# A hybrid streaming layer: four steps moved from VectorE to ScalarE and TensorE, and one set of weight parts made once

## The chip, the cores and the metric

The kernel runs on one core of a Trainium2 chip. The metric is the device time of one execution in microseconds (us). TensorE (PE in the profile) does the matmuls, VectorE (DVE), ScalarE (ACT) and GpSimd (POOL) the elementwise work; SyncE (SP) issues most of the DMAs. Each engine takes its own instructions in the order in which they were planned.

## What is computed

One layer of a streaming encoder in fp32, for 1024 prompt tokens and 8 running streams of 16 tokens each (1152 tokens in all, width 1024): RMSNorm, one input projection to three mixers, an output projection with a residual, RMSNorm, SwiGLU, a residual and a last RMSNorm. The mixers and the two parts that the change touches, cut:

```python
def rglru(x, h0, ...):                       # mixer A
    log_a = -LRU_C * r * softplus(-lam)
    a = exp(log_a)
    u = sqrt(-expm1(2.0 * log_a)) * (i * x)
    # h[t] = a[t] * h[t-1] + u[t]; then y = h * gelu(gate)

def ssd_chunk(s, inp):                       # mixer B
    acs = cumsum(da, axis=1)
    diff = acs[:, :, None] - acs[:, None]
    decay = exp(where(causal_mask, diff, -inf))
    cb = einsum("btgn,bsgn->btsg", cm, bm)
    y = einsum("btsg,btsgh,bsghp->btghp", cb, decay, x) + ...
    s_new = exp(acs[:, -1]) * s + einsum("bsgn,bsghp->bghpn", bm, x * tail)

def trunk_layer(x, ...):
    x = x + einsum("bte,ed->btd", mix, w_out)
    h2 = rmsnorm(x, norm2_w)                 # y * rsqrt(mean(x*x) + eps)
    ff = silu(h2 @ w_ffn_gate) * (h2 @ w_ffn_up)
    x = x + ff @ w_ffn_down
```

## The kernel before

Tokens lie in nine tiles of 128; tile 0 (`samp`) holds the eight running streams, tiles 1 to 8 the prompt. Three tiles are a chunk of 384 columns. Every fp32 operand of a large matmul is split into a high part (fp32r, copied by ACT) and a low part (the rest, a subtraction on DVE or POOL), and a product is three matmuls (`mm3`, L144 to L146). Weights come by `load_w` (L159 loads, L160 high part, L164 low part), or, in the feed-forward, by `a_parts`, where `split` (L179, L180) makes the parts and L1008 to L1011 combine blocks of the weights before.

The stages, in program order: the first norm and the input projection for all tokens; `mix_c` for each tile (mixer C); `mix_a` twice (mixer A, halves of its width); `proj_xbc` and `proj_z` (inputs of mixer B); then per chunk three times `mix_b` and, between them, `w_out` for the chunk (output projection, residual, squares for the second norm); then the feed-forward.

`mix_a` works on tiles of 128x1152. After an exponential (L358) and a tanh (L359) on ACT, L361 makes `0.5 t + 0.5` of the first on DVE, L362 to L365 go on, L367 makes `-2 t - 1` on DVE ahead of the scan. The gelu of the gate has one such step too (L381, `0.044715 t + 1`).

`mix_b` has for each of the two groups of four heads a tile `L` of 128x512 that a DMA fills with the cumulated decays along the free side (`ad`, broadcast). Four DVE instructions (L721), one for a head, subtract the decay of the partition's own token and cut at 0; ACT takes the exponential of all four (L722), DVE multiplies by the masked C B (L723). In the sample tile a loop over eight sequences follows: DVE copies a strip (`zw`, L734), two matmuls read the old state (`pi`), DVE masks B to the sequence (`bm`, L739, one buffer), two matmuls give the new contribution (`pn`, tag c of PSUM, three banks, of which `pi` holds two), POOL scales the old state (L743) and DVE adds (L744).

`w_out(c)` has eight output tiles of 24 matmuls of 384 columns (`pw`, two banks of tag a). For each, DVE adds the residual (L819), a DMA stores it, and `add_sq` takes the square on ACT (L216, L219) and adds it on DVE to a running sum (L220). After the eighth, `row_scale` sums over partitions by three matmuls of one column (`pss`), DVE and POOL take the power -1/2, and a matmul with a diagonal spreads it (`rrow`).

The feed-forward takes tokens in two sets, s = 1 (640 tokens, matmuls of 320 columns) and s = 0 (512 tokens, 256 columns), and hidden features in 11 pairs of tiles. Each block product is done in seven products instead of eight (Strassen's way), in this order: A11, S2, S3, S4, A12, S1, A22. `build(s)` makes the seven combinations of the tokens, first the high and low parts of three, then of four (L979, L984, L180). `build(1)` needs the first two chunks alone, `build(0)` needs the last. So pair 0 is done apart: `gate_up(0, (1,), "0a")`, `build(0)`, `gate_up(0, (0,), "0b")`; each call makes the gate's weight parts (g0a, g0b) and then the up's (u0a, u0b). Three buffers each hold high and low parts, so a set of parts takes the place of the one before as the products let go of it. From pair 1 on one set of parts serves both s. The down projection is last.

The order of the instructions on each engine is planned by a list scheduler on a simulated timeline; code under `feed()` or `high_priority` is taken ahead.

Of the kernel before, what the change touches and what calls it, by code (L numbers as in the profile page):

```python
# [18 lines left out]
P = 128  # L19
# [34 lines left out]
AE = dict(g0a="101", u0a="010", g0b="101", u0b="010")  # L54
# [36 lines left out]
def hybrid_step(ctx, tc, xT, xTp, vec, rows, nrow, wch, wtk0, wtk1, wout, wgate, wup, wdown,  # L91
# [28 lines left out]
    V.memset(cst[:, 2:3], float(np.exp(1.0)))  # L120
    ident, ones = cio[:, 0:P], cio[:, P:2 * P]
# [77 lines left out]
    def row_scale(rs, sq, c, name):  # L199

        load_cm()
        pc = bank("d", f"pss{name}", [TPC])
        for i in range(TPC):
            for j, x in enumerate(sq):
                mm(pc[:, i:i + 1], x[:, i * P:(i + 1) * P], ones[:, 0:1], j == 0, j == len(sq) - 1)
        rstd_from(rs, pc, D)
# [138 lines left out]
    def mix_a(j):  # L345
# [15 lines left out]
        V.tensor_scalar(t4, t4, 0.5, 0.5, ALU.mult, ALU.add)  # L361
# [5 lines left out]
        V.tensor_scalar(t3, t3, -2.0, -1.0, ALU.mult, ALU.add)  # L367
# [13 lines left out]
        V.tensor_scalar(t4, t4, 0.044715, 1.0, ALU.mult, ALU.add)  # L381
# [299 lines left out]
    def mix_b(t, last):  # L681
# [122 lines left out]
    def w_out(c):  # L804
        mT = st["mT", c]
        cs = slice(c * CH, (c + 1) * CH)
        sq = io.tile([P, CH], F32, tag="sq", name=f"sq2{c}", bufs=SQ)
        for m in range(KD):
# [14 lines left out]
        row_scale(r, [sq], c, f"2{c}")  # L823
# [71 lines left out]
    etb = pr.tile([P, NB, 8], F32, name="etb")  # L895

# [90 lines left out]
    def a_parts(w, pair, name, single):  # L987
# [34 lines left out]
    def gate_up(pair, ss, tag):  # L1022
        gt = {s: pg.tile([P, 2, 2, BN[s]], F32, tag=f"g{s}", name=f"g{s}_{tag}") for s in ss}
        for w, up in ((wgate, False), (wup, True)):
            nm = f"{'gu'[up]}{tag}"
            tm = {}
            for s in ss:
# [62 lines left out]
    for pair in range(1, NF // 2):  # L1090
        gate_up(pair, (0, 1), str(pair))
# [345 lines left out]
```

## Time and profile before

| | us |
|---|---|
| median of 3 runs (lowest to highest) | 1451.86 (1448.03 to 1453.65) |
| the profiled execution's own time | 1447.59 |
| its span in the trace | 1445.8 |
| busy in the span: TensorE, VectorE, ScalarE, GpSimd | 1349.6, 1082.0, 523.2, 527.2 |
| mean granted TensorE clock | 0.976 of full |

The span is the time between the first and the last instruction of the program; the rest of the execution's time lies around it. Matmuls are pipelined, so two of them overlap in the trace, and the step from one start to the next is what one costs in a row. Idle time of an engine is told with what ended it. TensorE's clock is granted at one of two levels, 1.2 or 2.4 GHz, and a stretch shows the mean as a share of the higher.

### The profile page before, as it was taken

How to read it: one execution, taken by the hardware profiler on the slowest of the kernel's cores; microseconds unless marked ns; L12 is line 12 of the kernel's file. 1: busy time of each engine (PE TensorE's matmuls, PEld its weight loads, DVE VectorE, ACT ScalarE, POOL GpSimd, SP SyncE). 2: the span in 40 equal slices, each digit the busy share in tenths (PEclk: the TensorE clock that was granted, in tenths of full speed). 3: DMA queues.
4: the chain of work that ended last, by engine and by line, in shares of the span. 5: the costliest groups of instructions: out<-in, count | busy, mean ns of one | idle time of the engine just before them, and what ended most of it. 6: DMA issues, size and time to landing. Idle time of an engine off the chain costs nothing.

```text
span 1445.8 us, 24385 instructions
## 1 busy us (share of the span) xinstructions
PE 1349.6 (93%) x9341; PEld 1299.9 (90%) x9341; DVE 1082.0 (75%) x2016; ACT 523.2 (36%) x895; POOL 527.2 (36%) x419
## 2 busy tenths in 40 slices
PE   8998998999988899787899999999999999999986
PEld 7898887899987799787899999999999999998885
DVE  8475697988777697689556666565666688999896
ACT  7332255444533145464322231232222453333222
POOL 4160032211014332213543454544545433452453
PEclk9999999999999999988999999999999999999998
DMA  6263131433466887750412322223322363544523
GB/s 236 77 209 125 42 101 52 125 106 103 135 221 215 274 280 257 235 188 30 153 47 99 117 102 102 69 78 116 103 100 90 111 208 109 178 134 127 166 66 131
DMA packets 107289, 195.82 MB, mean 135 GB/s; under 512 B 10845, under 2 KB 66597, under 8 KB 107045
## 3 DMA queue, kind: packets, MB, share of 16 engines
q1 hardware_dynamic: 102276, 186.40, 39.0%
q0 software_dynamic: 4896, 7.87, 1.9%
q8 instruction: 73, 1.20, 0.3%
q14 instruction: 44, 0.35, 0.1%
HBM read 137.82 MB, written 56.41 MB: 134 GB/s over the span
## 4 chain that ended last, share of the span: by engine, by line
PE 53%; DVE 27%; DMA 9%; issue 5%; ACT 3%; POOL 3%; SPq 0%; DVEq 0%; POOLq 0%; ACTq 0%
PE pS_g L144 3%; PE pS_u L144 3%; PE pS_u L145 3%; PE pS_g L146 3%; PE pS_g L145 3%; PE pS_u L146 3%; PE pA_u L144 2%; PE pA_u L146 2%; PE pA_u L145 2%; PE pA_g L145 2%; PE pA_g L144 2%; PE pA_g L146 2%; DVE as L180 2%; PE pmb L145 2%; PE pmb L144 2%
## 5 line engine op out<-in xcount | busy, mean ns | idle before, releaser
L144 PE MATMUL pd<-e,as 128*128 128x256 f32 (+1 forms) x560 | 167.3, 301 | 9.8 <-ACT as L179 4.7
L146 PE MATMUL pd<-e,as 128*128 128x256 f32 (+1 forms) x560 | 162.6, 298 | 3.1 <-DVE as L180 3.1
L145 PE MATMUL pd<-e,as 128*128 128x256 f32 (+1 forms) x560 | 165.1, 296 | 0.0
L144 PEld LDWEIGHTS pd<-e,as 128*128 128x128 f32 x560 | 106.4, 190 | 14.2 <-ACT as L179 6.1
L180 POOL TENSOR_TENSOR al_u<-wr_u,ah_u 128x1024 fp32r<-128x1024 f32 x30 | 72.1, 2404 | 117.1 <-ACT ah_u L179 117.1
L146 PEld LDWEIGHTS pd<-e,as 128*128 128x128 f32 x560 | 105.3, 190 | 4.7 <-DVE as L180 4.6
L145 PEld LDWEIGHTS pd<-e,as 128*128 128x128 f32 x560 | 105.9, 189 | 0.1
L180 POOL TENSOR_TENSOR al_g<-wr_g,ah_g 128x1024 fp32r<-128x1024 f32 x30 | 71.9, 2396 | 90.5 <-ACT ah_g L179 89.8
L179 ACT ACTIVATE ah_g<-wr_g 128x1024 fp32r<-128x1024 f32 x30 | 31.8, 1062 | 150.8 <-PE pS_u L145 80.4
L1046 POOL TENSOR_TENSOR g<-g,pt_u 128x256 f32<-128x256 f32 (+1 forms) x80 | 76.9, 980 | 20.3 <-DVE pt_u L1045 15.4
L146 PE MATMUL pA_g<-b,al_g 128*128 128x256 f32 (+1 forms) x240 | 71.5, 299 | 1.6 <-POOL al_g L180 1.6
L144 PE MATMUL pw<-mT,wh_o 128*128 128x384 f32 x192 | 67.5, 354 | 4.9 <-DVE xr L819 4.2
L144 PE MATMUL pA_g<-b,ah_g 128*128 128x256 f32 (+1 forms) x240 | 71.6, 298 | 0.4 <-ACT ah_g L179 0.4
L145 PE MATMUL pA_g<-b,ah_g 128*128 128x256 f32 (+1 forms) x240 | 71.5, 298 | 0.0
L144 PE MATMUL pS_g<-b,ah_g 128*128 128x256 f32 (+1 forms) x240 | 70.9, 296 | 0.5 <-ACT ah_g L179 0.5
L144 PE MATMUL pA_u<-b,ah_u 128*128 128x256 f32 (+1 forms) x240 | 71.0, 296 | 0.0
L146 PE MATMUL pA_u<-b,al_u 128*128 128x256 f32 (+1 forms) x240 | 70.8, 295 | 0.0
L144 PE MATMUL pS_u<-b,ah_u 128*128 128x256 f32 (+1 forms) x240 | 70.6, 295 | 0.0
L145 PE MATMUL pA_u<-b,ah_u 128*128 128x256 f32 (+1 forms) x240 | 70.6, 294 | 0.0
L145 PE MATMUL pS_g<-b,ah_g 128*128 128x256 f32 (+1 forms) x240 | 70.6, 295 | 0.0
L146 PE MATMUL pS_u<-b,al_u 128*128 128x256 f32 (+1 forms) x240 | 70.5, 294 | 0.0
L145 PE MATMUL pS_u<-b,ah_u 128*128 128x256 f32 (+1 forms) x240 | 70.4, 294 | 0.0
(725 smaller groups left out, 4779.2 us busy)
## 6 DMA issues: line engine op xcount, KB each, us to landing
wr_o<-in_dram SPq DMA_DIRECT2D x24, 512.0 KB, 4.9
wr_g<-in_dram SPq DMA_DIRECT2D x20, 512.0 KB, 3.5
wr_u<-in_dram SPq DMA_DIRECT2D x20, 512.0 KB, 3.5
wd<-in_dram SPq DMA_DIRECT2D x15, 512.0 KB, 4.2
wr_t<-in_dram SPq DMA_DIRECT2D x14, 512.0 KB, 3.6
fr<-ffd SPq DMA_DIRECT2D x11, 640.0 KB, 4.0
ffd<-g SPq DMA_DIRECT2D x10, 640.0 KB, 2.9
ffd<-g SPq DMA_DIRECT2D x10, 512.0 KB, 3.0
```

The costliest lines, as they stand in the source:

```text
L144: T.matmul(out, ah, bh, start=start, stop=False)
L145: T.matmul(out, ah, bl, start=False, stop=False)
L146: T.matmul(out, al, bh, start=False, stop=stop)
L179: S.activation(dst_hi, src, AF.Copy)
L180: eng.tensor_tensor(dst_lo, src, dst_hi.bitcast(F32), ALU.subtract)
L1046: G.tensor_tensor(g, g, u, ALU.mult)
```

## The change

Five edits.

1. In `mix_b` the decay differences are made by ACT: `relu(acs - L)`, with the token's own decay as the bias per partition, and the exponential takes the scale -1.
2. In the sample tile's loop B is masked twice ahead of the loop, once for the even and once for the odd sequences (`par`), and the matmul for a sequence reads the 32 rows in which it and its neighbour lie.
3. In `mix_a` the three steps L361, L367 and L381 go to ACT as `Identity` with a bias.
4. In `w_out` of the last chunk each square goes into one of two buffers, and three matmuls of one column add it in PSUM, in a bank for each of the three token tiles (one of tag b, two of c); the running sum on DVE goes.
5. In pair 0 the order is now gate for s = 1, up for s = 1, `build(0)`, up for s = 0 with the same weight parts, gate for s = 0. So u0b, its loads and its parts go, and the gate's silu for s = 0 comes after the up.

```diff
-        V.tensor_scalar(t4, t4, 0.5, 0.5, ALU.mult, ALU.add)
+        S.activation(t4, t4, AF.Identity, bias=cst[:, 1:2], scale=0.5)
...
-        V.tensor_scalar(t3, t3, -2.0, -1.0, ALU.mult, ALU.add)
+        S.activation(t3, t3, AF.Identity, bias=cst[:, 3:4], scale=-2.0)
...
-        V.tensor_scalar(t4, t4, 0.044715, 1.0, ALU.mult, ALU.add)
+        S.activation(t4, t4, AF.Identity, bias=ones[:, 0:1], scale=0.044715)
...
-                V.tensor_scalar(L[:, h, :], L[:, h, :], acs[:, hh:hh + 1], 0.0, ALU.subtract, ALU.min)
-            S.activation(L, L, AF.Exp)
+                S.activation(L[:, h, :], L[:, h, :], AF.Relu, bias=acs[:, hh:hh + 1], scale=-1.0)
+            S.activation(L, L, AF.Exp, scale=-1.0)
...
         if samp:
+            bm = [pr.tile([P, 2, P], F32, tag=("ke", "oc")[e], name=f"bm{e}") for e in range(2)]
+            for e in range(2):
+                V.tensor_scalar(bm[e], Bt, par[:, e:e + 1], None, ALU.mult)
             for b in range(NB):
                 s0 = st["s0f"][:, b, :]
+                rs = slice(b // 2 * 32, b // 2 * 32 + 32)
...
-                bm = pr.tile([P, 2, P], F32, tag="ke", name=f"bm{b}")
-                V.tensor_scalar(bm, Bt, seqm[:, b:b + 1], None, ALU.mult)
                 pn = bank("c", f"pn{b}", [8, 64])
                 for g in range(2):
-                    mm(pn[:, g * 4:g * 4 + 4, :], bm[:, g, :], xq[:, g * 4:g * 4 + 4, :])
+                    mm(pn[:, g * 4:g * 4 + 4, :], bm[b % 2][rs, g, :], xq[rs, g * 4:g * 4 + 4, :])
...
+        if c == NCHUNK - 1:
+            pcs = [bank("bcc"[i], f"pss2{c}{i}", [1]) for i in range(TPC)]
...
                 V.tensor_tensor(xr, xr, pm, ALU.add)
                 dma(x1d[:, m, cs], xr)
-                add_sq(sq, xr, m, f"2{c}", V)
+                if c == NCHUNK - 1:
+                    tq = io.tile([P, CH], F32, tag=("tq", "sq")[m % 2], name=f"tq2{c}_{m}", bufs=1)
+                    S.activation(tq, xr, AF.Square)
+                    for i in range(TPC):
+                        mm(pcs[i], tq[:, i * P:(i + 1) * P], ones[:, 0:1], m == 0, m == KD - 1)
+                else:
+                    add_sq(sq, xr, m, f"2{c}", V)
...
             def out(s, i, h, x, pm):
                 g, u = gt[s][:, i, h, :], tm[s][0]
-                if up:
-                    V.tensor_tensor(u, x, pm, ALU.add)
+                o = u if second else g
+                V.tensor_tensor(o, x, pm, ALU.add)
+                if not up:
+                    S.activation(o, o, AF.Silu)
+                if second:
                     G.tensor_tensor(g, g, u, ALU.mult)
-                else:
-                    V.tensor_tensor(g, x, pm, ALU.add)
-                    S.activation(g, g, AF.Silu)
...
+            for sp in sps:
+                second = sp[0] in gt
+                if up and pair == 0 and sp == (0,):
+                    build(0)
...
-    gate_up(0, (1,), "0a")
-    build(0)
-    gate_up(0, (0,), "0b")
+    gate_up(0, ((0, "g0a", ((1,),)), (1, "u0a", ((1,), (0,))), (0, "g0b", ((0,),))))
     for pair in range(1, NF // 2):
-        gate_up(pair, (0, 1), str(pair))
+        last = pair == NF // 2 - 1
+        gate_up(pair, ((0, f"g{pair}", ((0, 1),)), (1, f"u{pair}", ((0,), (1,)) if last else ((0, 1),))))
```

## Rows read from the trace of the kernel before

**Rows 1.** The page's first part: busy time, share, instructions.
```profile
PE 1349.6 (93%) x9341; PEld 1299.9 (90%) x9341; DVE 1082.0 (75%) x2016; ACT 523.2 (36%) x895; POOL 527.2 (36%) x419
```
**Rows 2.** Busy us by stretch: length, PE PEld DVE ACT POOL, clock, DMA share, GB/s.
```profile
180.00:290.00 110.00, 99.90 (x572) 89.35 (x572) 99.14 (x184) 59.10 (x117) 29.66 (x32) 0.95 0.31 94
396.00:440.00 44.00, 39.85 (x327) 38.53 (x326) 32.93 (x81) 17.40 (x39) 6.36 (x7) 1.00 0.70 233
440.00:490.00 50.00, 38.18 (x229) 32.42 (x227) 39.49 (x75) 10.72 (x21) 22.09 (x21) 1.00 0.70 228
490.00:598.00 108.00, 101.41 (x596) 96.74 (x596) 77.89 (x158) 46.38 (x90) 33.18 (x35) 0.97 0.86 277
598.00:640.00 42.00, 32.63 (x175) 31.52 (x173) 41.16 (x53) 24.43 (x37) 5.04 (x2) 0.94 0.50 160
640.00:704.00 64.00, 51.72 (x332) 50.09 (x332) 52.94 (x78) 27.87 (x39) 28.42 (x14) 0.85 0.29 103
704.00:1250.00 546.00, 543.46 (x4070) 542.35 (x4071) 362.43 (x617) 163.25 (x268) 260.14 (x171) 1.00 0.32 107
```
**Rows 3.** Waits of PE, 598 to 724 us: us in total, times, longest.
```profile
PE pss L139 <- DVE sq L220: 6.5, 1, 6.5
PE pS_u0a L144 <- ACT ah_u0a L179: 5.3, 1, 5.3
...
PE pS_g0b L146 <- DVE s1p_g0b L180: 2.4, 1, 2.4
PE pS_g0b L144 <- ACT ah_g0b L179: 1.9, 1, 1.9
...
PE pS_u0b L144 <- ACT ah_u0b L179: 1.1, 1, 1.1
PE pS_u0b L146 <- DVE s1p_u0b L180: 0.9, 1, 0.9
```
**Rows 4.** Busy time by stretch: sum of six at the lower clock.
```profile
sum 34.13, PE 27.30 PEld 27.00 DVE 26.27 ACT 10.94 POOL 13.66; mean PE 4.55 PEld 4.50 DVE 4.38 ACT 1.82 POOL 2.28
```
**Rows 5.** Groups of instructions, DVE, 598 to 704 us: busy, mean ns, idle before.
```profile
L220 DVE TENSOR_TENSOR sq<-sq,tq 128x384 f32<-128x384 f32 x7 | 3.9, 552 | 0.0
```
**Rows 6.** Timeline, DVE, 665 to 685 us: start, us, instruction.
```profile
665.49 0.68 DVE L1008 TENSOR_TENSOR s_g0b<-wr_g0b 128x512 f32<-128x512 f32 x1
...
680.54 2.83 DVE L180 TENSOR_TENSOR s1p_g0b<-s_g0b,s1p_g0b 128x512 fp32r<-128x512 f32 x1
683.69 1.21 DVE L180 TENSOR_TENSOR b<-xb,b 128x1024 fp32r<-128x1024 f32 x1
```
**Rows 7.** Timeline, PE, 702 to 703 us: two matmuls in a row.
```profile
702.42 0.28 PE L144 MATMUL pA_u0b<-b,ah_u0b 128*128 128x256 f32 x1
702.54 0.28 PE L145 MATMUL pA_u0b<-b,ah_u0b 128*128 128x256 f32 x1
```
**Rows 8.** Timeline, PE, 57 to 60 us: the one-column matmuls of a chunk.
```profile
57.44 0.72 PE L139 MATMUL pss<-cio,xk 128*128 128x1 f32 x6
```
**Rows 9.** Waits of PE, 396 to 612 us.
```profile
PE pn L139 <- DVE bm L739: 5.0, 5, 1.7
...
PE ptz L145 <- DVE wl_t L164: 3.1, 1, 3.1
```
**Rows 10.** Line L739: count, duration in ns (min/median/max), first and last start.
```profile
L739 DVE TENSOR_SCALAR bm<-ws,cm x8: 341/348/1448, 447.0 to 486.5; 128x256 f32<-128x256 f32 x8
```
**Rows 11.** Timeline, DVE, 404 to 407 us: four heads, with the wait before.
```profile
404.75 0.87 DVE L721 TENSOR_SCALAR ws<-ws,sml 128x128 f32<-128x128 f32 x4 [3.62 <-DMA ws<-acd]
```
**Rows 12.** Timeline, ACT, 176 to 184 us: two in a row with bias.
```profile
182.50 0.69 ACT L561 ACTIVATE ke<-ldq 128x128 f32<-128x128 f32 x2
```
**Rows 13.** Line L361 on DVE: count, duration in ns, first and last start.
```profile
L361 DVE TENSOR_SCALAR a<-a x2: 751/754/756, 185.4 to 233.7; 128x1152 f32<-128x1152 f32 x2
```
**Rows 14.** Groups by form, ACT: an affine step with exponential.
```profile
L358 ACT ACTIVATE a<-a,sp 128x1152 f32<-128x1152 f32 x2 | 2.7, 1342 | 0.0
```
**Rows 15.** Groups by form, ACT: the table loads of L364.
```profile
L364 ACT ACT_TABLE_LOAD x2 | 2.6, 1283 | 0.0
```

More of the change, by code (lines that the diff above doesn't have):

```diff
@@ L53 @@
 SEQ = "4abcd7856"
-AE = dict(g0a="101", u0a="010", g0b="101", u0b="010")
+AE = dict(g0a="101", u0a="010", g0b="101")
 SEN = ((1, 0), (1, 0), (1, 0))
@@ L120, in hybrid_step @@
     V.memset(cst[:, 2:3], float(np.exp(1.0)))
+    V.memset(cst[:, 3:4], -1.0)
     ident, ones = cio[:, 0:P], cio[:, P:2 * P]
@@ L201, in row_scale @@
         load_cm()
[L202 to L206, printed above, removed]
+        if sq is None:
+            powc(rs, rs, 0)
+        else:
+            pc = bank("d", f"pss{name}", [TPC])
+            for i in range(TPC):
+                for j, x in enumerate(sq):
+                    mm(pc[:, i:i + 1], x[:, i * P:(i + 1) * P], ones[:, 0:1], j == 0, j == len(sq) - 1)
+            rstd_from(rs, pc, D)
         dg = io.tile([P, CH], F32, tag="tq", name=f"dg{name}", bufs=TQ)
@@ L806, in w_out @@
         cs = slice(c * CH, (c + 1) * CH)
-        sq = io.tile([P, CH], F32, tag="sq", name=f"sq2{c}", bufs=SQ)
+        if c == NCHUNK - 1:
+            pcs = [bank("bcc"[i], f"pss2{c}{i}", [1]) for i in range(TPC)]
+        else:
+            sq = io.tile([P, CH], F32, tag="sq", name=f"sq2{c}", bufs=SQ)
         for m in range(KD):
@@ L895, in hybrid_step @@
     etb = pr.tile([P, NB, 8], F32, name="etb")
+    par = pr.tile([P, 2], F32, name="par")
+    V.tensor_reduce(par, seqm.rearrange("p (i e) -> p e i", e=2), mybir.AxisListType.X, ALU.add)
     f0, f1, q0 = first_tiles(("f0", "f1", "q0"), ws)
@@ L985, in build, with a_parts @@
             split(b_part(s, k, 0, 3, 4), b_part(s, k, 1, 3, 4), t, V)
-    def a_parts(w, pair, name, single):
+    def a_parts(w, pair, name):
         def pairs(src, nm, eng=G):
@@ L1020, in a_parts, with gate_up @@
                     A22=half(g1, 1), S2=half(g2, 0), S4=half(g2, 1))
[L1022 to L1027, printed above, removed]
-                tm[s] = [pg.tile([P, BN[s]], F32, tag=f"pt{s}{j}", name=f"pt{s}{j}_{nm}") for j in range(3)]
-            A = a_parts(w, pair, nm, len(ss) == 1)
+    def gate_up(pair, steps):
+        gt, tm = {}, {}
+        for up, nm, sps in steps:
+            A = a_parts((wgate, wup)[up], pair, nm)
             def prod(a, b, s):
-                tags = "abcabcc" if tag == "0a" else "abcabcdc"
+                tags = "abcabcc" if pair == 0 and s == 1 else "abcabcdc"
                 pm = bank(tags[pcount[0] % len(tags)], f"p{a}{s}_{nm}", [BN[s]])
@@ L1043, in out @@
                 g, u = gt[s][:, i, h, :], tm[s][0]
-                if up:
-                    V.tensor_tensor(u, x, pm, ALU.add)
-                    G.tensor_tensor(g, g, u, ALU.mult)
-                else:
-                    V.tensor_tensor(g, x, pm, ALU.add)
-                    S.activation(g, g, AF.Silu)
-            for sp in ((0,), (1,)) if up and pair == NF // 2 - 1 else (ss,):
+                o = u if second else g
[3 more added lines that the diff above has]
+                if second:
+                    G.tensor_tensor(g, g, u, ALU.mult)
+            for sp in sps:
+                second = sp[0] in gt
+                if up and pair == 0 and sp == (0,):
+                    build(0)
+                for s in sp:
+                    if not second:
+                        gt[s] = pg.tile([P, 2, 2, BN[s]], F32, tag=f"g{s}", name=f"g{s}_{pair}")
+                    tm[s] = [pg.tile([P, BN[s]], F32, tag=f"pt{s}{j}", name=f"pt{s}{j}_{nm}") for j in range(3)]
                 for s in sp:
@@ L1068, in gate_up @@
                     out(s, 1, 0, tm[s][2], prod("A22", T4, s))
-        for s in ss:
+        for s in gt:
             n, o = BN[s], 7 * BO[s] // 2
```

9 lines of the change are left out of this document (8 added, 1 removed).

## The prediction

> **What bounds the kernel now.** I read the page's busy times first: TensorE (PE) is busy for 1349.6 us of a span of 1445.8 us [rows 1], so at most 96 us can be won without taking work from it. The second view is the table of busy time by stage. It says where those 96 us lie: between 704 and 1250 us PE idles for 2.5 us of 546, so nothing that eases another engine there is worth anything, while the mixers' stretch at 180 to 290 us idles for 10, the SSD tiles at 396 to 440 for 4, the stretch with the sample tile at 440 to 490 for 12, 490 to 598 for 7, the last output projection at 598 to 640 for 9 and the first feed-forward pair at 640 to 704 for 12 [rows 2]. VectorE (DVE) is busy for 41.2 of 42 us in 598 to 640, and for 52.9 of 64 after it; ScalarE (ACT) is busy there for under 60%. So in the stretches that the change touches PE waits for DVE. The third view names the waits of the last two stretches: 6.5 us for the running sum of squares, 5.3 for weight parts of u0a, 2.4 and 1.9 for those of g0b, 1.1 and 0.9 for those of u0b [rows 3]. The fourth is the granted clock after such waits: six stretches between 591 and 711 us, 34.1 us in all, ran at the lower of its two levels (1.2 GHz), with PE busy for 27.3 us of them [rows 4]; at 2.4 GHz that work would have taken about half, so the low clock costs up to 13.7 us, on top of the idle time.
>
> **The squares of the last output projection and the up weights once.** These two edits meet in one stretch, 598 to 704 us. First what leaves DVE: seven additions of squares at 0.552 us are 3.9 us [rows 5]. In `gate_up` the parts of g0b come, before, between those of u0a and the last split of `build(0)`, which ends at 684.9 us: six DVE instructions, the first and the last of them shown, 0.68 + 0.67 + 1.21 + 0.68 + 0.67 + 2.83 = 6.7 us [rows 6]. After, the second half of u0a's products comes first and holds the same buffers, so g0b's parts can only be made behind `build(0)`. DVE is full up to there, so the last split moves forward by 3.9 + 6.7 = 10.6 us, to 674.3. What PE still has to do then: products of 12 matmuls at 0.12 us, the step between two starts [rows 7], are 1.4 us each; six of the seven of u0a's second half (the first needs only the early half of `build(0)`) are 8.6 us, seven of g0b 10.1, and one change of weights, priced like that into u0b, 1.1 + 0.9 = 2.0 [rows 3]. That ends at 674.3 + 20.7 = 695.0, where pair 1 starts at 704 now: 9 us less. The u0b parts themselves (two loads of 512 KB, seven or eight instructions on DVE, as many on ACT and POOL) fall away as well, but lay in a stretch where DVE had room, so I count nothing for them.
>
> What is added: each of eight output tiles gets three one-column matmuls in place of three at the end. Six records, which are three such matmuls, take 0.72 us in a row and start 0.1 us apart [rows 8], so a tile costs about 0.6 us and the whole 8 x 0.6 - 0.6 = 4.2 us; at the lower clock twice that. They lie in a stretch where PE idles for 9 us [rows 2], so most is covered; I count +1, bounded by 0 and +8.4. The squares are no longer chained to one buffer and DVE, so the 6.5 us wait at the end shrinks to one addition, one square and the matmuls; this is how the DVE time becomes an earlier `rrow`, and is not counted twice. PE's queue is in order, so behind a square's matmul stands the next output tile: that is the rival below. The three accumulators hold one bank of tag b and two of c until the end; only the first product of g0a could want them earlier, and it fits in what is left. **Sum for this stretch: -9 + 1 = -8 us**; from below all idle time and the low clock there could close (9.4 + 12.3 - 4.2, some 17 us, without counting the clock), from above +5.
>
> **Two masks for B.** Of the PE waits in 396 to 612 us, 5.0 us, five times, are for the masked B of the sample tile [rows 9], one DVE instruction of 0.348 us in the median for each of eight sequences [rows 10], in a loop where each waits for the buffer that the last matmul frees. After, two masks are made ahead. What is late next is the single free bank of tag c: the next `pn` waits for the state's addition on DVE, which stood ahead of the mask. So 8 x 0.35 = 2.8 us of chain go, less two masks ahead, and the other half of the wait stays: **-2.5 us**, bounds 0 and -5. The matmul now takes 32 rows in place of 128; no row shows its price for 256 columns, and I take the present one.
>
> **The decay differences on ACT.** Per half of a tile four DVE instructions take 0.87 us, and the same row shows DVE standing 3.62 us for their DMA [rows 11]. ACT's nearest form, 128x128 with a bias per partition, takes 0.69 us for two [rows 12], so 0.30 more for each further one and 1.29 for four. For 18 halves DVE gives up 18 x 0.8 = 14.4 us and ACT takes on 18 x 1.2 = 21.6. One handover between engines goes, and 0.42 us of run time comes in each half. The wait for the DMA moves with the work: now ACT stands in it, and queued behind are the weights' high parts (L160) and the tanh that empties a PSUM bank of `z` (L462), for which PE waits in turn; before, the low parts of weights stood there, at 3.1 us in one wait [rows 9]. PE idles for 11 us in 396 to 440 and 490 to 598 together [rows 2]. I take **-1.5 us**, bounds -5 and +7.6 (18 x 0.42, if each half is on the path).
>
> **Three RG-LRU steps on ACT.** Six DVE instructions at 0.75 us become six on ACT whose nearest rows take 1.34 us [rows 13, 14]: DVE gives up 4.5 us in a stretch where it is busy for 90% [rows 2], ACT takes on 8, and each chain is 0.6 us longer. Nothing soon waits for these chains; their result goes to DRAM. **-0.6 us**, bounds -4.5 and +3.6.
>
> For both moves the Trainium skill speaks against the change: the rules for kernel authors of "ScalarE: Activation LUTs" put `relu`, `add` and `mul` on VectorE and not on ScalarE. The trace agrees that each is dearer on ACT (0.30 against 0.2 us, 1.34 against 0.75); the result that this rule would give is the second rival.
>
> **The sum**, against the profiled execution's span: 1445.8 - 8 - 2.5 - 1.5 - 0.6 = 1433.2 us, and 1435.0 beside its own time of 1447.59. The median of the runs shown is 4.3 us above that execution, so I forecast 1435.0 + 4.3 = **1439 us**.
>
> **Rivals.** (1) *Everything closes.* If PE never stops between 598 and 704 us, the stretch gives -17 in place of -8, and a clock kept at 2.4 GHz through half of [rows 4] a few more: about 1428. For it: the waits name exactly what is edited. Against: DVE stays nearly full even without 10.6 us. (2) *ACT becomes the late one*, and the gain is handed back: 18 x 0.42 + 6 x 0.6 = 11.2 us of longer chains eat the 12.6, and the time is about 1450, no change. For it: ACT stands in its queue for the same late DMA. Against: ACT is busy for 10.7 of 50 us and 46.4 of 108 in those stretches [rows 2]. This is what the skill's rule quoted above would make of it. (3) *Slower: PE stands for the squares.* A tile's matmuls need its addition on DVE and its square on ACT, two steps of about 0.55 us by the addition of the same shape [rows 5]. If the order puts them ahead of the next tile's product, PE waits for 1.1 us eight times, 8.8 us, works 4.2 to 8.4 more, and the forecast's -12.6 turns into +0.4 to +4.6, and into +10 if DVE's queue (up to one wait of 6.5 us [rows 3]) is behind it as well: about 1459. It decides once a square comes later than the next product's 3.8 us (24 matmuls of 384 columns, 0.16 us by scaling [rows 7]). (4) *Relu needs a table of its own*: two loads at 1.283 us [rows 15] for each of 18 halves, 46 us slower, about 1498. No row shows Relu. The skill's "ScalarE: Activation LUTs", on table sets, says that cheap functions such as relu are in every set; no run here shows that yet.
>
> **How the numbers follow.** Forecast 50%, rival 1 12%, rival 2 with everything near no change 22%, rival 3 13%, rival 4 3%. A measurement of this kernel tells some 0.5% (7.3 us) from no change. The forecast's own cases, from 1431 to 1445, lie almost whole on the fast side: faster 0.62, same 0.22, slower 0.16. The range goes from rival 1 almost to rival 3: 1427 to 1457.
>
> **What would show it.** Right: no wait of PE for `sq`, the last split of `build(0)` some 10 us earlier against the end of the projection, one wait for weights less before pair 1, no wait of `pn` for `bm`, and pair 1 starting 10 to 13 us earlier. Wrong: waits of PE for `tq2` or for the `z` banks with ACT as the releaser, more table loads on ACT, or products of u0a's second half standing for `build(0)` as long as g0b's did. Since the order of all engines is planned anew, a change in 704 to 1446 us by over 3 us would also make the sum wrong.

## The result, and the profile after

The changed kernel takes 1438.95 us in the median (1436.49 to 1440.48), the kernel before, measured beside it, 1452.12: a ratio of 0.9908, 95% interval 0.9888 to 0.9929. The forecast of 1439 holds. The parts of the sum don't: three of its terms are off, in directions that cancel, and most of what follows is about that.

The page of the changed kernel begins with the busy times, as [rows 1] did for before:

```profile
PE 1362.8 (95%) x9383; PEld 1311.7 (91%) x9383; DVE 1048.0 (73%) x1923; ACT 544.5 (38%) x969; POOL 523.1 (36%) x417
```

DVE gave up 34 us and ACT took on 21. PE is *busier*, in a shorter span (1437.3 us): its idle time fell by 21.7 us (96.2 to 74.5), but it has 4 us of new one-column matmuls, and some 9 us more of its busy time are lost to the lower clock, as the sums further down show. The table by stage (columns as in [rows 2]) shows where:

```profile
180.00:290.00 110.00, 100.61 (x566) 88.51 (x565) 92.61 (x180) 65.30 (x130) 30.58 (x31) 0.92 0.32 94
396.00:440.00 44.00, 41.36 (x331) 39.32 (x331) 29.20 (x56) 24.90 (x64) 6.56 (x8) 1.00 0.75 239
440.00:490.00 50.00, 46.86 (x274) 39.84 (x274) 31.75 (x57) 16.22 (x39) 21.47 (x21) 0.89 0.77 262
490.00:598.00 108.00, 98.55 (x580) 94.08 (x579) 74.52 (x119) 53.61 (x119) 30.55 (x33) 0.97 0.87 273
598.00:640.00 42.00, 39.15 (x218) 38.43 (x217) 35.25 (x44) 22.69 (x31) 6.67 (x3) 0.91 0.47 154
640.00:704.00 64.00, 54.88 (x379) 52.90 (x379) 55.13 (x86) 29.18 (x44) 26.96 (x15) 0.92 0.32 105
704.00:1250.00 546.00, 545.59 (x4115) 544.72 (x4114) 363.12 (x622) 166.97 (x272) 259.07 (x171) 1.00 0.33 109
```

From 598 to 704 us PE idles for 12.0 us, where it idled for 21.7 [rows 2]. In 440 to 490 us it is busy for 46.9 us in place of 38.2, but its granted clock in that stretch fell from 1.00 to 0.89; from 479.3 us on it runs at the lower level, where about 4.8 of these 8.7 us are lost again.

The waits of PE from 598 to 724 us (us in total, times, longest), against [rows 3]:

```profile
PE pA_u0a L146 <- DVE b L181: 4.2, 2, 3.4
...
PE pS_u0a L145 <- ACT ah_u0a L180: 1.3, 1, 1.3
PE pA_g L147 <- POOL al_g L181: 1.1, 1, 1.1
...
PE pS_g0b L147 <- DVE s1p_g0b L181: 0.9, 1, 0.9
...
PE pss L140 <- ACT tq L835: 0.2, 1, 0.2
```

The 6.5 us wait for the sum of squares is 0.2 now, and the 5.3 us for parts of u0a are 1.3. PE waits for a part of `build(0)` instead, 4.2 us. After these waits two stretches, 595.3 to 605.5 and 660.2 to 670.4 us, run at the lower clock, where there were six; their sum, beside [rows 4]:

```profile
sum 20.40, PE 15.10 PEld 14.45 DVE 11.30 ACT 5.13 POOL 5.85; mean PE 7.55 PEld 7.23 DVE 5.65 ACT 2.56 POOL 2.92
```

**Where the time went.** Two marks divide the trace: the first matmul of the last chunk's output projection, and the first of pair 1. Their rows in the timeline of PE (start, us, instruction), before and then in the changed kernel:

```profile
581.89 0.34 PE L144 MATMUL pw<-mT,wh_o 128*128 128x384 f32 x1
...
704.09 0.39 PE L144 MATMUL pA_g<-b,ah_g 128*128 128x256 f32 x1 [0.43 <-ACT ah_g L179]
```

```profile
587.04 0.34 PE L145 MATMUL pw<-mT,wh_o 128*128 128x384 f32 x1
...
698.56 0.28 PE L145 MATMUL pA_g<-b,ah_g 128*128 128x256 f32 x1
```

So the changed kernel reaches the first mark 5.15 us later, needs 111.52 us from there to the second in place of 122.20 (-10.68), and 738.7 us from there to the end of the span in place of 741.7 (-3.0). That makes the 8.5 us by which the spans differ. The medians differ by 13.2 us, because the profiled execution of before is 4.5 us under the median measured beside the changed kernel, and that of after lies on its own median. How the +5.15 us is to be read is settled by the first experiments.

### The profile page after: what moved, and what is told of

Read it like the earlier page. It is cut to its first block, busy times and chain, and to the rows that moved or that the text cites. A ratio compares the mean times of both kernels' runs of the same rounds, so it can differ in the third digit from the quotient of the medians.

```text
span 1437.3 us, 24425 instructions
## 1 busy us (share of the span) xinstructions
PE 1362.8 (95%) x9383; PEld 1311.7 (91%) x9383; DVE 1048.0 (73%) x1923; ACT 544.5 (38%) x969; POOL 523.1 (36%) x417
## 4 chain that ended last, share of the span: by engine, by line
PE 37%; DVE 13%; DMA 6%; POOL 2%; issue 2%; ACT 1%; SPq 0%; DVEq 0%; POOLq 0%; ACTq 0%
PE pS_g L145 3%; PE pS_u L145 3%; PE pS_g L147 3%; PE pS_u L146 3%; PE pS_g L146 3%; PE pS_u L147 3%; PE pA_u L147 2%; PE pA_u L145 2%; PE pA_u L146 2%; PE pA_g L146 2%; PE pA_g L145 2%; PE pA_g L147 2%; PE pd L145 2%; PE pd L146 2%; PE pd L147 2%
## 5 line engine op out<-in xcount | busy, mean ns | idle before, releaser
L145 PE MATMUL pw<-mT,wh_o 128*128 128x384 f32 x192 | 68.1, 357 | 6.1 <-DMA mT<-mixd 4.0
L146 PE MATMUL pw<-mT,wh_o 128*128 128x384 f32 x192 | 67.9, 354 | 3.3 <-DMA mT<-mixd 3.3
L145 PE MATMUL pS_u<-b,ah_u 128*128 128x320 f32 (+1 forms) x240 | 70.5, 295 | 0.0
L146 PE MATMUL pS_u<-b,ah_u 128*128 128x256 f32 (+1 forms) x240 | 70.3, 294 | 0.0
```

The lines of the kernel that those rows point to most:

```text
L145: T.matmul(out, ah, bh, start=start, stop=False)
L146: T.matmul(out, ah, bl, start=False, stop=False)
```

## The experiments

The first question was which of the five edits carries the gain. Four kernels took before and made one part, or the two that meet in one stretch. Where a difference is given in us beside a ratio, it is the ratio's, taken of the median of before that was measured with it; for the whole change that is 13.4 us.

**Squares on TensorE and up weights once** (edits 4 and 5, the others as before):

```diff
...
+                    for i in range(TPC):
+                        mm(pcs[i], tq[:, i * P:(i + 1) * P], ones[:, 0:1], m == 0, m == KD - 1)
...
+    gate_up(0, ((0, "g0a", ((1,),)), (1, "u0a", ((1,), (0,))), (0, "g0b", ((0,),))))
...
```

> The kernel before with the squares of the last projection on TensorE and the up weights' parts made once; the three edits in the mixers are left out. The forecast priced these two at -8 us together, so about 0.9945 of before. The trace of the changed kernel says more: pair 1 starts there 5.5 us earlier although the last projection starts 5.2 us later, so the two would give -11 to -13 us, about 0.992. If instead the gain of the changed kernel comes from the mixers, this kernel is within 4 us of before.

Measured: 0.9919 (0.9901 to 0.9937), 11.8 us less (13.3 by the medians). Nearly the whole gain is here.

**Decay differences on ACT alone** (edit 1):

```diff
-                V.tensor_scalar(L[:, h, :], L[:, h, :], acs[:, hh:hh + 1], 0.0, ALU.subtract, ALU.min)
-            S.activation(L, L, AF.Exp)
+                S.activation(L[:, h, :], L[:, h, :], AF.Relu, bias=acs[:, hh:hh + 1], scale=-1.0)
+            S.activation(L, L, AF.Exp, scale=-1.0)
```

> The kernel before with the decay differences alone on ScalarE. Forecast: -1.5 us. Rival, ScalarE becomes the late one: 18 halves of 0.42 us, up to +7.6 us, with waits of TensorE for the z banks or for weights' parts that ScalarE releases. The changed kernel, which is some 5 us behind before when the last projection starts, allows either.

Measured: 0.9998 (0.9984 to 1.0013): nothing.

**The masks alone** (edit 2):

```diff
...
-                    mm(pn[:, g * 4:g * 4 + 4, :], bm[:, g, :], xq[:, g * 4:g * 4 + 4, :])
+                    mm(pn[:, g * 4:g * 4 + 4, :], bm[b % 2][rs, g, :], xq[rs, g * 4:g * 4 + 4, :])
...
```

> The kernel before with the two masks for B alone. Forecast: -2.5 us, since five waits for the mask (5.0 us) go. Rival from the trace of the changed kernel, where the clock was granted at the lower level for 13.7 us from 479 us on although TensorE was busy: the waits go, the clock falls instead, and the sum is 0 to +4 us.

Measured: 1.0073 (1.0054 to 1.0092), 10.6 us *slower* (8.8 by the medians), where the forecast had 2.5 us less.

**RG-LRU steps alone** (edit 3):

```diff
...
-        V.tensor_scalar(t4, t4, 0.5, 0.5, ALU.mult, ALU.add)
+        S.activation(t4, t4, AF.Identity, bias=cst[:, 1:2], scale=0.5)
...
```

> The kernel before with the three RG-LRU steps alone on ScalarE. Forecast: -0.6 us, with bounds of -4.5 and +3.6. Rival from the trace of the changed kernel: between 260 and 380 us three new stretches at the lower clock stand there (6.8, 3.4 and 3.4 us), so that the steps on ScalarE delay the mixers of B and C by +4 to +8 us.

Measured: 1.0008 (0.9991 to 1.0025): nothing.

The second question: which of the two feed-forward edits it is, whether the masks cost in the whole change too, and whether their 32 rows are the reason.

**Squares alone** (edit 4):

```diff
...
-                add_sq(sq, xr, m, f"2{c}", V)
...
+                    S.activation(tq, xr, AF.Square)
+                    for i in range(TPC):
+                        mm(pcs[i], tq[:, i * P:(i + 1) * P], ones[:, 0:1], m == 0, m == KD - 1)
...
```

> The kernel before with the squares of the last projection alone on TensorE. By the forecast's sum DVE gives up 3.9 us ahead of the last split of build(0) and TensorE takes on 1 (0 to 8.4): about -3 us. The wait of TensorE for the running sum (6.5 us) goes in any case. Rival: the matmuls of one column hold up the next output tile, and the time is the same or up to 5 us longer.

Measured: 1.0039 (1.0026 to 1.0053), 5.7 us slower. The wait that the edit aims at is gone, and PE waits elsewhere. Its waits in 598 to 724 us:

```profile
PE pS_u0a L144 <- ACT ah_u0a L179: 8.8, 1, 8.8
PE pS_g0b L146 <- POOL al_g0b L180: 4.8, 1, 4.8
...
PE pss L139 <- ACT tq L831: 0.2, 1, 0.2
```

The timelines of DVE and ACT in this kernel show where u0a's weights stand, and so how the 5.3 us wait of [rows 3] became 8.8:

```profile
653.52 8.52 DVE L998 TENSOR_TENSOR xb<-xb,rrow 128x1024 f32<-128x1024 f32 x4
...
667.64 0.68 DVE L1030 TENSOR_TENSOR wx<-wx 128x512 f32<-128x512 f32 x1
```

```profile
668.41 2.00 ACT L179 ACTIVATE ah_u0a<-wx 128x1024 fp32r<-128x1024 f32 x2 [5.17 <-DVE wx L1030]
```

The earlier `rrow` lets four scalings of `xb` start together, 8.52 us on DVE in a row; the steps that make u0a's weights stand behind them in the same queue, and the high part on ACT and PE behind those. Counted from the first mark, PE comes to this product 5.5 us earlier than before (69.2 us in place of 74.7), but the last DVE step of its weights ends only 2.1 us earlier (76.8 for 78.9), so the wait grows. The changed kernel has such a row of 8.51 us too and waits for these weights for only 1.3 us: with edit 5 PE has u0a's product for s = 0 to do in between, and stands 4.2 us for its `b` instead.

**Up weights once, alone** (edit 5):

```diff
...
-    gate_up(0, (1,), "0a")
-    build(0)
-    gate_up(0, (0,), "0b")
+    gate_up(0, ((0, "g0a", ((1,),)), (1, "u0a", ((1,), (0,))), (0, "g0b", ((0,),))))
...
```

> The kernel before with the up weights' parts made once, alone. By the forecast's sum 6.7 us of DVE work move behind build(0) and one change of weights goes: -6 to -7 us. If the two edits of the feed-forward only help together, this one gives under 3 us; if it carries all, -11 us as both did together (0.9919).

Measured: 0.9930 (0.9916 to 0.9944), 10.2 us less. This one edit is most of the change. The wait for the sum of squares stays, at 5.9 us.

**What the stretch between the two marks consists of** is one row for each kernel: before, changed, both edits, up weights alone, squares alone. In each the columns are the stretch, its length, busy time of PE, PEld, DVE, ACT and POOL, clock, DMA share, GB/s.

```profile
581.89:704.09 122.20, 95.34 (x550) 91.30 (x549) 99.66 (x143) 57.06 (x85) 35.28 (x18) 0.87 0.45 150
```

```profile
587.04:698.56 111.52, 95.33 (x591) 92.17 (x591) 93.27 (x135) 53.18 (x79) 31.26 (x16) 0.91 0.45 146
```

```profile
586.37:699.46 113.09, 98.13 (x591) 94.15 (x591) 95.88 (x136) 52.91 (x79) 29.89 (x16) 0.89 0.44 143
```

```profile
587.16:700.16 113.00, 93.53 (x550) 90.01 (x549) 94.38 (x138) 52.66 (x79) 32.46 (x17) 0.89 0.45 147
```

```profile
591.56:715.12 123.56, 97.93 (x592) 94.12 (x591) 98.69 (x141) 57.28 (x85) 39.44 (x20) 0.89 0.44 147
```

Length less PE's busy time is idle time. Of the busy time, what lies at the lower clock (23.9 us before, 20.7 with the up weights alone, 20.0 with both edits and with the squares alone, 15.1 in the changed kernel) counts half as work and half as lost clock. Worked out so:

| kernel | length | work at full clock | lost to the clock | PE idle |
|---|---|---|---|---|
| before | 122.2 | 83.4 | 11.9 | 26.9 |
| up weights once | 113.0 | 83.2 | 10.4 | 19.5 |
| both edits | 113.1 | 88.1 | 10.0 | 15.0 |
| squares | 123.6 | 87.9 | 10.0 | 25.6 |
| changed kernel | 111.5 | 87.8 | 7.6 | 16.2 |

The squares add 4.5 us of work to PE, or 4.9 on top of the up weights. Alone they close 1.3 us of idle time; beside the up weights they close 4.5 and so come out even. The up weights close 7.4 us of idle time and add no work.

The same sum for everything ahead of the first mark rests on these two rows, before and then changed:

```profile
0.00:581.89 581.89, 539.88 (x3473) 503.71 (x3474) 445.01 (x898) 243.91 (x459) 150.06 (x158) 0.98 0.50 161
```

```profile
0.00:587.04 587.04, 553.69 (x3474) 514.66 (x3474) 421.29 (x815) 268.51 (x537) 150.63 (x158) 0.96 0.51 160
```

All kernels start the same 3473 matmuls ahead of that mark, and with half of the busy time at the lower clock taken off they come to 528 to 531 us of work in each of them, which is a test of the halving. Before idles for 42.0 us there and loses 9.1 to the clock; the changed kernel idles for 33.3 and loses 22.3.

The same rows answer what the +5.15 us at the first mark are. The three kernels of the last three edits have the order of before, instruction by instruction on every engine, up to at least 598 us, and reach the first mark at 586.37, 587.16 and 591.56 us: 4.5, 5.3 and 9.7 us after the profiled execution of before. So a start at 587.04 is no loss of the changed kernel; it lies among executions of the same work. Ahead of that mark the three idle for 39.2 to 46.3 us and lose 14.7 to 17.0 to the clock, so the profiled execution of before was one that had kept its clock. One thing stays open here: of the 5.7 us that the squares cost alone, the stretch between the marks shows 1.4, and the rest lies ahead of the first mark, where the order is that of before. Single traces can't weigh the mixers' edits to better than about 5 us, and the ratios have to.

**All but the masks** (edits 1, 3, 4 and 5):

```diff
...
-            bm = [pr.tile([P, 2, P], F32, tag=("ke", "oc")[e], name=f"bm{e}") for e in range(2)]
-            for e in range(2):
-                V.tensor_scalar(bm[e], Bt, par[:, e:e + 1], None, ALU.mult)
...
+                bm = pr.tile([P, 2, P], F32, tag="ke", name=f"bm{b}")
+                V.tensor_scalar(bm, Bt, seqm[:, b:b + 1], None, ALU.mult)
...
```

> The changed kernel with the loop of before in the sample tile: eight masks, matmuls over 128 rows. The masks alone made the kernel before 10.6 us slower. If that cost lies in the loop and its clock, it is in the changed kernel too, and this kernel is 3 to 10 us faster than the changed one (about 0.985 of before). If it lies in how the planned order of the masks alone fell out between 520 and 610 us, this kernel is within 3 us of the changed one (0.989 to 0.993).

Measured: 1436.54 us, 0.9892 (0.9878 to 0.9906). By the ratios the change is 2.3 us better without its masks, but the intervals overlap: the masks earn nothing that shows.

**Changed kernel with 128 rows in the masked product:**

```diff
-                    mm(pn[:, g * 4:g * 4 + 4, :], bm[b % 2][rs, g, :], xq[rs, g * 4:g * 4 + 4, :])
+                    mm(pn[:, g * 4:g * 4 + 4, :], bm[b % 2][:, g, :], xq[:, g * 4:g * 4 + 4, :])
```

> The changed kernel with the two masks, but each new contribution to the state is a matmul over all 128 rows instead of 32; so it adds up four sequences where one is wanted, and the sample streams' new state of mixer B is left out in this sense. Masks, waits and counts of instructions are the same. Theory: the 32 rows are why the clock was granted at the lower level for 13.7 us from 479 us on; then this stretch is gone here and the kernel is 3 to 7 us faster than the changed one. Rival: the clock falls for the loop's order, whatever the rows; then the stretch and the time stay as in the changed kernel.

Measured: 0.9885 (0.9870 to 0.9900), 3.3 us under the changed kernel, the intervals again overlapping. The trace shows a difference at one place. Sample tile, 480 to 495 us: first a window of the changed kernel cut to its low-clock stretch, then the window in this one (columns as above).

```profile
479.30:492.90 13.60, 12.57 (x38) 9.79 (x38) 6.99 (x13) 1.48 (x6) 5.69 (x7) 0.50 1.13 358
```

```profile
480.00:495.00 15.00, 12.31 (x75) 11.24 (x74) 9.03 (x16) 5.23 (x18) 9.37 (x11) 1.00 1.17 385
```

With 32 rows 13.6 us run at the lower level (1.2 GHz), half of whose 12.6 busy us, 6.3 us, is clock lost. With 128 rows the clock is 1.00, and 75 matmuls start in 15 us where 38 did in 13.6. It is not that PE had idled more ahead of it: from 440 to 480 us it is busy for 37.9 of 40 us with 32 rows and for 36.4 with 128. Nor is it the order: PE's instructions are the same in the two kernels up to 485 us in this one and 495 us in the changed one. But all but the masks, with 128 rows as well, has 10.2 us at the lower level at the same place (from 480.5 us), so the rows aren't shown to be the cause.

**Masks alone with 128 rows** (the edit against the masks alone):

```diff
-                    mm(pn[:, g * 4:g * 4 + 4, :], bm[b % 2][rs, g, :], xq[rs, g * 4:g * 4 + 4, :])
+                    mm(pn[:, g * 4:g * 4 + 4, :], bm[b % 2][:, g, :], xq[:, g * 4:g * 4 + 4, :])
```

> The kernel before with the two masks alone, as in the run of the masks alone (10.6 us slower than before), but with matmuls over all 128 rows, so that the sample streams' new state of mixer B adds up four sequences. Theory: the 32 rows and the lower clock behind them carry that loss; then this kernel is within 4 us of before or faster, and the clock at 482 us stays at the higher level. Rival: the loss is the new order between 520 and 610 us; then it is 6 to 12 us slower than before here too.

Measured: 1.0033 (1.0013 to 1.0052), against 1.0073 with 32 rows: about half of the loss goes with the rows. The other 4.8 us remain with masks of full height, between the two outcomes that were named. In the traces, one execution each, most of it lies between the two marks, well behind the sample tile: 126.6 us here and 126.1 with 32 rows, for 122.2 before.

```profile
590.39:716.95 126.56, 95.77 (x550) 90.69 (x549) 98.90 (x143) 57.39 (x85) 36.39 (x19) 0.88 0.44 144
```

**All but the masks and the squares** (edits 1, 3 and 5):

```diff
...
-                    tq = io.tile([P, CH], F32, tag=("tq", "sq")[m % 2], name=f"tq2{c}_{m}", bufs=1)
-                    S.activation(tq, xr, AF.Square)
-                    for i in range(TPC):
-                        mm(pcs[i], tq[:, i * P:(i + 1) * P], ones[:, 0:1], m == 0, m == KD - 1)
...
+                add_sq(sq, xr, m, f"2{c}", V)
...
```

> Decay differences and RG-LRU steps on ScalarE and the up weights' parts once, with the squares summed on VectorE and eight masks as before. It tells what the squares on TensorE are worth in the whole: with them this kernel took 0.9892 of before. The up weights alone took 0.9930. If the squares are worth the forecast's 3 us, this kernel is at 0.991 to 0.993; if they gain nothing beside the other edits, at 0.988 to 0.990.

Measured: 0.9908 (0.9877 to 0.9940), as the whole change, and 2.3 us above the kernel with the squares (0.9892), with wide intervals that overlap: nothing that the squares or the masks earn beside the other edits shows, and neither outcome named for the squares is settled.

**The eight masks made by ACT, in two buffers, 128 rows** (with edits 1, 3, 4 and 5):

```diff
...
+                bm = pr.tile([P, 2, P], F32, tag=("ke", "oc")[b % 2], name=f"bm{b}")
+                S.activation(bm, Bt, AF.Copy, scale=seqm[:, b:b + 1])
...
```

> All edits but the masks; instead each of the eight masks is made by ScalarE, alternately into two buffers, and the matmuls keep 128 rows. The wait for the mask's one buffer goes as with the two masks, without 32 rows. If that wait was worth something by itself, this kernel is 1 to 3 us under the one with eight masks on VectorE (0.9892 of before); if the next wait in the loop takes its place, the two are equal within 2 us.

Measured: 1436.85 us, 0.9891 (0.9863 to 0.9920). The wait for `bm` is gone from the waits of PE and the clock in 480 to 495 us is 1.00, yet the time is that of the kernel that makes the masks on DVE as before. This doesn't price the 5.0 us of [rows 9], though, for that wait had nearly gone without any edit to the masks. Here it is in the same window with eight masks on DVE, first in all but the masks, then in the decay differences alone:

```profile
PE pn L140 <- DVE bm L744: 1.2, 1, 1.2
```

```profile
PE pn L139 <- DVE bm L739: 0.9, 2, 0.5
```

So edits 1 and 2 aim at one wait, and with the decay differences off DVE most of it is gone. The transfers of `mT`, for which PE waits 6.7 us here, cost 6.5 in all but the masks too.

**All but the decay differences** (edits 2 to 5):

```diff
-                S.activation(L[:, h, :], L[:, h, :], AF.Relu, bias=acs[:, hh:hh + 1], scale=-1.0)
-            S.activation(L, L, AF.Exp, scale=-1.0)
+                V.tensor_scalar(L[:, h, :], L[:, h, :], acs[:, hh:hh + 1], 0.0, ALU.subtract, ALU.min)
+            S.activation(L, L, AF.Exp)
```

> The change without the decay differences on ACT: masks, RG-LRU steps, squares and up weights once. Alone, the masks cost +0.0073 (10.6 us), the decay differences -0.0002; with everything together the masks cost only 0.0016 (0.9908 against 0.9892 without them). Theory A: the 14 us that the decay differences take off VectorE are what covers the masks in the whole; without them the masks cost what they cost alone, and the sum of the single effects holds: 0.9919 + 0.0073 + 0.0008 = 1.000, about 1452 us, and at least 0.995. Theory B: the decay differences earn nothing beside the others either, and the masks' loss belongs to the order planned for them alone: 0.990 to 0.993, within 3 us of the whole change. Between 0.993 and 0.995 neither is shown.

Measured: 1444.68 us, 0.9949 (0.9929 to 0.9968). That lies at the edge between the two bounds: the sum of the single effects (1.000) lies above the interval, and the whole change's 0.9908 below it, their two intervals just touching. So neither theory holds as it stood: beside the masks the decay differences on ACT seem to be worth some 6 us, though alone they are worth nothing. One place where the traces differ: PE, behind 590 us, waits for the mixer's last output on DVE, in this kernel and then in the masks alone:

```profile
PE pmb L790 <- DVE wb L786: 5.3, 1, 5.3
```

```profile
PE pmb L785 <- DVE wb L781: 3.7, 1, 3.7
```

In the changed kernel this wait is 0.7 us. But before has it with 3.1 us, and so has the 128-row change, which is as fast as any, so it doesn't carry the 6 us. The clock differs more: ahead of the first mark PE idles for 33.3 us in this kernel as in the changed one, and loses 27.7 us to the lower clock in place of 22.3, with 17.1 us at that level in the sample tile, from 476.3 us on. That is one execution of each; the cause of the 6 us stays open.

## Why the total was right and its terms were not

The forecast came true with the help of luck: one term was too small by about 3 us and another too large by about as much.

**The stretch with the squares and the up weights: -8 forecast, -10.7 in the trace, -11.8 by the ratio of both edits.** The mechanism named for the up weights is right, and two of its steps are mis-sized in opposite directions.

The first is "g0b's parts can only be made behind `build(0)`", 6.7 us of DVE. The timeline of DVE in the changed kernel shows that most of them are not:

```profile
666.67 0.68 DVE L1033 TENSOR_TENSOR s_g0b<-wr_g0b 128x512 f32<-128x512 f32 x1
...
671.93 0.68 DVE L1034 TENSOR_TENSOR wr_g0b<-wr_g0b,wr_g0b 128x512 f32<-128x512 f32 x1
...
673.94 1.22 DVE L181 TENSOR_TENSOR al_g0b<-wr_g0b,ah_g0b 128x1024 fp32r<-128x1024 f32 x1
...
676.41 0.68 DVE L1035 TENSOR_TENSOR wr_g0b<-s_g0b,wr_g0b 128x512 f32<-128x512 f32 x1
...
678.88 0.68 DVE L1036 TENSOR_TENSOR wr_g0b<-wr_g0b 128x512 f32<-128x512 f32 x1
...
680.28 3.49 DVE L181 TENSOR_TENSOR b<-xb,b 128x1024 fp32r<-128x1024 f32 x3
...
686.50 2.45 DVE L181 TENSOR_TENSOR s1p_g0b<-s_g0b,s1p_g0b 128x512 fp32r<-128x512 f32 x1
```

Five of the six still come ahead of the last split (680.28 + 3.49 = 683.77); they write buffers that u0a's products don't hold. Only the one at 686.50, 2.83 us before [rows 6], moved. So the last split should come 3.9 + 2.8 = 6.7 us earlier against the first mark, not 10.6, and it came 6.3 earlier: 683.77 - 587.04 = 96.7 us, where before had 684.90 - 581.89 = 103.0. With the up weights alone, where the 3.9 us of squares stay, it is 3.3.

The second is the tail behind the last split, put at 20.7 us because only the first of the seven products of u0a's second half could go ahead of it. In the changed kernel 54 of their 84 matmuls had started by then: each takes a split as it comes, and all but the products that read the last one need not wait. The 30 that were left are 3.6 us, the 84 of g0b with their change of weights (0.95 us, where 2.0 was priced) 11.1, and pair 1 starts 14.8 us after the last split. Before it was 19.2. The two errors, 4.3 us too much (10.6 against 6.3) and 5.9 too little (20.7 against 14.8), leave more than the forecast: 6.3 + 4.4 = 10.7. In the time of the trace pair 1 starts 5.5 us earlier, not the 10 to 13 that were to show it, since the first mark came 5.15 us later.

**The squares** were priced at -3.9 us of DVE and +1 us of PE. DVE's part came: counted from the first mark, the last split moves 1.4 to 3.0 us more with them than without beside the up weights, and `rrow` 2.1 to 3.0; alone they move by 7.5 and 5.5. But alone PE then needs 28.1 us from the last split to pair 1 in place of 19.2, since it has stood for u0a's weights by then and still stands for g0b's, 4.8 us; and beside the up weights the 4.5 us of idle time that close are the size of the 4.9 us of new work. And "most is covered" failed: the 4.2 us of matmuls are the size that was worked out from [rows 8],

```profile
611.17 0.72 PE L140 MATMUL pss<-cio,tq 128*128 128x1 f32 x6
```

but the cover that they use is the idle time that they were to remove. Alone they lose 5.7 us. Rival 3, in which PE stands for each square, did not occur (0.2 us in all); a loss for the edit alone did, in part by another way, DVE's queue, where the row of 8.52 us stands.

**Idle time and clock.** The low clock was left out of the forecast and kept for rival 1. Of the -10.7 us, 4.3 came from it (11.9 to 7.6 in the table), 10.7 from idle time, and 4.4 were given back as work of the squares. So the stretch got part of what rival 1 promised.

**The mixers together: -4.6 forecast, about nothing by the ratios** (13.4 us for the whole less 11.8 for the two feed-forward edits, each to some 3 us). The forecast counted idle time of PE, and that did close. The window from 396 to 612 us, before and then changed (columns as above):

```profile
396.00:612.00 216.00, 191.69 (x1213) 179.07 (x1211) 163.99 (x322) 82.71 (x159) 66.67 (x64) 0.98 0.75 246
```

```profile
396.00:612.00 216.00, 199.44 (x1238) 185.58 (x1238) 142.72 (x240) 100.27 (x230) 59.43 (x62) 0.94 0.79 255
```

DVE is relieved of 21 us and PE is busy for 7.8 us more, but at 0.94 of the clock in place of 0.98, which is some 8 us of a 200 us load. Ahead of the first mark the sum is the same: before and the three kernels of its order idle there for 42 us and lose 14 to the clock in the mean, the changed kernel 33.3 and 22.3, so what the mixers' edits close, some 9 us, comes back as some 8 of lost clock. Since the clock was left out of the sum for the mixers, this is the step that failed there. And the projections now wait longer for their input, a transfer (waits of PE in the same stretch; before it was 1.3 us):

```profile
PE pw L145 <- DMA mT<-mixd: 4.0, 2, 3.0
PE pw L146 <- DMA mT<-mixd: 3.3, 2, 1.9
```

**The masks: -2.5 forecast, +10.6 us alone, about +2 in the whole.** The step that failed in the whole change is the 5.0 us wait taken as it stood in before: beside the decay differences about 1 us of it is left (the two rows above). The step that held is the next wait: after, PE's wait for `bm` is replaced by one for the state's addition. In the changed kernel, 396 to 612 us:

```profile
PE pn L140 <- DVE s0f L752: 1.7, 2, 0.9
```

The price of the 32-row matmul, "I take the present one", held for one at the higher clock, but the clock was left out here too. The groups by form say 454 ns for one against 396 before, and 379 ns for forms with 128 rows:

```profile
L140 PE MATMUL pn<-ws,bm 32*128 32x256 f32 x32 | 10.5, 454 | 1.7 <-DVE s0f L752 1.7
L140 PE MATMUL pn<-ws 128*128 128x256 f32 x12 | 3.1, 379 | 0.0
```

The mean is higher because part of them ran at the lower clock; the fastest took 374 ns, so fewer rows save nothing. The three kernels with 32 rows (the changed one, the masks alone, all but the decay differences) have low-clock stretches of 13.6, 10.2 and 17.1 us between 476 and 494 us. With 128 rows there is none from 440 to 500 us in before, in the two feed-forward edits together, in the 128-row change and in the ACT masks; 1.7 to 6.9 us in the squares, the up weights, the decay differences, the RG-LRU steps (each alone) and the masks with 128 rows; and 10.2 us in all but the masks (from 480.5 us) and in the kernel without masks and squares (from 478.3 us), each beginning within a wait of 3.1 or 3.2 us for `mT`. These two had kept PE busy for 5.8 and 5.7 of the 8 us ahead; but the 128-row change, busy for 5.4 of the 8 us from 472 on, kept its clock, and the changed kernel, busy for 7.1 of the 8 us ahead, did not. So neither the rows nor idle time tells these traces apart, and why the clock falls there stays open. By the ratios the rows cost 5.8 us in the masks alone (intervals just apart) and 3.3 in the whole change (intervals overlapping). Since the order was planned anew for the 128 rows as well, from 490 us on, this is the price of the rows with their order. Why the masks with 128 rows still lose 4.8 us is not settled: PE's order differs from before's from 472 us on, and its wait for `wb` is 4.1 us at its longest, but no run took that order alone.

**The decay differences: -1.5 forecast, 0 alone, -6 beside the masks.** The price of the step was right, 1.27 us for four (22.9 us in all) where 1.29 were priced:

```profile
L726 ACT ACTIVATE wb<-wb,sml 128x128 f32<-128x128 f32 x40 | 12.6, 390 | 11.0 <-DMA wb<-acd 11.0
L726 ACT ACTIVATE ws<-ws,sml 128x128 f32<-128x128 f32 x32 | 10.3, 390 | 10.1 <-DMA ws<-acd 9.9
```

ACT now stands in the wait for the DMA that DVE stood in, 20.9 us in all (18.1 on DVE before), as forecast. The low parts on DVE stand for it in turn (`wl_o` behind ACT's `wh_o`, 11.9 us in 396 to 598 us, for 5.5 before), and no wait of PE for `wl_o` shows.

**The RG-LRU steps: -0.6 forecast, 0 measured.** 1.25 us each on ACT, for 1.34 priced. Rivals 2 and 4: ACT did not become the late engine, and no table load was added. The Trainium skill's rule in "ScalarE: Activation LUTs" (rules for kernel authors), that such steps belong on VectorE, holds for each instruction here (390 ns against some 280, 1.25 us against 0.75) and, alone, for the result, which gained nothing; beside the masks the run without the decay differences on ACT took 6 us longer, which the rule would not give. What the same page of the Trainium skill says on table sets, that relu and identity are in every set, agrees with the eight loads both before and after.

**The rest.** From pair 1 to the end the span is 3.0 us shorter, 2.1 of it PE's idle time in 704 to 1250 us (2.5 before [rows 2], 0.4 after). The forecast named this, a change by over 3 us, as what would spoil its sum; it lies at that limit and was not in it. And the +4.3 us from the profiled execution to the median fits what the traces show at the first mark, which kernels of the same order reach 4.5 to 9.7 us later. One reading of the prediction needs a word: the stretches that it names hold 57 of the 96 us of idle time; the rest lies ahead of 180 us and behind 1250 us, where no edit works.

So the sum reads, forecast against what the runs support: feed-forward -8 and -10.7 to -11.8; the mixers -4.6 and -1.6, with an error of some 3 us; the rest 0 and up to -3.

## What to carry to other kernels

Before an edit takes instructions off an engine, ask for each one that is to move which buffer really holds it back, and count for the engine behind it how much of its work is already free to run: both were misjudged here, and the errors happened to cancel. Idle time that closes is not yet time won: beside it, read the granted clock of the same stretch before and after. Work put on the bounding engine is free only where the idle time around it is not the very idle time the edit is meant to remove. Price each edit alone and beside the others, and ask whether two of them aim at the same wait: here one of five carried the gain, the masks lost 0.7% alone and 0.2%, within the error, in company, and the decay differences were worth nothing alone and seemed worth 0.4% in company.

## What the runs showed of the hardware

- A matmul that reads 32 rows took 374 ns at the higher clock, one with 128 rows 377 to 379: fewer rows made it hardly cheaper. With them in the sample tile the granted clock fell to its lower level for 13.6 us while PE was busy for 12.6 of those, and in the masks alone for 10.2 us with PE busy for all of it (the row below). Two kernels with 128 rows have 10.2 us at the lower level there as well, so the rows are not shown to be the reason.

```profile
482.20:492.40 10.20, 10.20 (x28) 7.84 (x27) 1.38 (x2) 0.00 (x0) 0.00 (x0) 0.50 0.77 241
```

- Three fp32 matmuls of one column are six records that start 0.11 us apart and took 0.72 us together; records of 256 columns of the split operands start 0.12 us apart [rows 7], so one column was hardly cheaper.
- Half of PE's busy time at the lower clock counts as lost: with that taken off, the same 3473 matmuls come to 528 to 531 us in all kernels of this case, though the share lost runs from 9.1 to 27.7 us.
- Kernels with the same order up to 598 us reached the last projection at 581.9 to 591.6 us, one execution each: the spread of executions is as large as the gain of this change, and only ratios over several runs tell edits of the mixers apart.
